# Channel shuffle: load and store buffers 3 + 2 against 2 + 3, with the first load and store buffer shared by the three small tiles

## Chip, cores, metric

One NeuronCore of a Trainium2 chip. The metric is the device time of the kernel in microseconds.

## The reference

`x` has shape (16, 64, 64, 256) in float32, `groups` is 8. Within each pixel the 256 channels are a matrix of 8 groups by 32 channels, and it is transposed. Nothing is calculated.

```python
def reference(x, groups):
    batch, h, w, c = x.shape
    x = x.reshape(batch, h, w, groups, c // groups)
    x = x.transpose(0, 1, 2, 4, 3)
    return x.reshape(batch, h, w, c)
```

67.11 MB are read and 67.11 MB written, whatever the kernel does.

## The kernel before

Each of the 128 partitions takes `q` pixels of 1 KB per tile, so a tile of 38 is a load of 38 KB a partition (4864 KB), one VectorE copy that permutes, and one store. Loads are issued by SyncE, stores by ScalarE. Small tiles of 4, 8 and 16 come first, so that the first store starts early.

```python
_SIZES = [4, 8, 16] + [38] * 12 + [28]
_IN_BUFS = 3
_OUT_BUFS = 2
# ... (pools of _IN_BUFS and _OUT_BUFS buffers)
    for q in _SIZES:
        in_tile = in_pool.tile([P, biggest * c], F32, name="in_tile")
        nc.sync.dma_start(out=in_tile[:, : q * c], in_=rows(x_flat, first, q))
        out_tile = out_pool.tile([P, biggest * c], F32, name="out_tile")
        nc.vector.tensor_copy(
            out=out_tile[:, : q * c].rearrange("p (i j g) -> p i j g", j=CPG, g=G),
            in_=in_tile[:, : q * c].rearrange("p (i g j) -> p i j g", g=G, j=CPG),
        )
        nc.scalar.dma_start(out=rows(out_flat, first, q), in_=out_tile[:, : q * c])
        first += P * q
```

Of the kernel before, what the change touches and what calls it, by code (L numbers as in the profile page):

```python
# [1 line left out]

# [4 lines left out]


F32 = mybir.dt.float32
P = 128  # L10

_SIZES = [4, 8, 16] + [38] * 12 + [28]
_IN_BUFS = 3
_OUT_BUFS = 2


@with_exitstack
def kernel(
    ctx: ExitStack,
    tc: tile.TileContext,  # L20
    x: bass.AP,
    groups: bass.AP,
    out: bass.AP,
):
    nc = tc.nc
    b, h, w, c = x.shape
    G = int(groups)
    CPG = c // G
    assert G * CPG == c
    assert sum(_SIZES) * P == b * h * w  # L30
    biggest = max(_SIZES)

    x_flat = x.rearrange("b h w c -> (b h w c)")
    out_flat = out.rearrange("b h w c -> (b h w c)")

    in_pool = ctx.enter_context(tc.tile_pool(name="in_pool", bufs=_IN_BUFS))
    out_pool = ctx.enter_context(tc.tile_pool(name="out_pool", bufs=_OUT_BUFS))

    def rows(flat, first, q):

        return flat[first * c : (first + P * q) * c].rearrange("(p f) -> p f", p=P)

    ctx.enter_context(tc.manual_schedule(engines=None))
    first = 0
    for q in _SIZES:
        in_tile = in_pool.tile([P, biggest * c], F32, name="in_tile")
        nc.sync.dma_start(out=in_tile[:, : q * c], in_=rows(x_flat, first, q))  # L47
        out_tile = out_pool.tile([P, biggest * c], F32, name="out_tile")
        nc.vector.tensor_copy(  # L49
            out=out_tile[:, : q * c].rearrange("p (i j g) -> p i j g", j=CPG, g=G),  # L50
            in_=in_tile[:, : q * c].rearrange("p (i g j) -> p i j g", g=G, j=CPG),
        )
        nc.scalar.dma_start(out=rows(out_flat, first, q), in_=out_tile[:, : q * c])
        first += P * q


# [1 line left out]
_INS = ['x', 'groups']  # L58
_OUTS = [((16, 64, 64, 256), 'float32')]

_NUMBERS = {'groups': 8}


# [26 lines left out]
```

## Time and profile before

| | before |
|---|---|
| time, median of the first 3 runs | 317.06 us (316.93 to 317.13) |
| span of the profiled run | 314.7 us |
| busy VectorE | 119.2 us, 38% |
| DMA engines, loads + stores | 49.8% + 49.4% of 16 engines' span |
| one round (one load, copy and store of 38 KB) | 23.0 us |

The page's DMA issues: tile and tensor, engine, count, KB each, median us from issue to landing.

```profile
in_tile<-in_x_dram SPq DMA_DIRECT2D x12, 4864.0 KB, 46.8
out_dram<-out_tile ACTq DMA_DIRECT2D x12, 4864.0 KB, 37.0
```

And the third copy (16 KB) in the timeline: start, length, instruction, and in brackets the idle time ahead of it with what ended it.

```profile
20.36 3.90 DVE L49 COPY out_tile<-in_tile 128x4096 f32<-128x4096 f32 x1 [11.75 <-DMA out_dram<-out_tile]
```

Its load had landed by 12.6 us (from the landings in the trace); it waited nearly 8 us more for an output buffer. This is the kind of wait that the change aims at.

### The profile page before, as it was taken

The page shows a single profiled execution, that of the slowest core. Times are in us where ns is not written, and L with a number is a line of the kernel's source. Part 1 is how long each engine was busy: PE and PEld are TensorE (multiplying, and loading weights), DVE is VectorE, ACT ScalarE, POOL GpSimd, SP SyncE. Part 2 cuts the span into 40 slices and gives each one's busy share as a digit, 9 for nine tenths or more (in the row PEclk, how much of TensorE's full clock was granted, in tenths as well). Part 3 has the DMA queues.
Part 4 walks back from the last instruction along what each step waited for, and adds up shares of the span by engine and source line. Part 5 has one row for each costly group of instructions (what it writes and reads, how often), then busy time and mean ns, then how long its engine had stood idle before and what let it go on. Part 6 is the DMA issues. An engine that isn't in the chain of part 4 may idle for free.

```text
span 314.7 us, 133 instructions
## 1 busy us (share of the span) xinstructions
DVE 119.2 (38%) x16; POOL 0.2 (0%) x4
## 2 busy tenths in 40 slices
DVE  3040645505506407407308209109109019046620
POOL 0000000000000000000000000000000000000000
DMA  8999999999999999999999999999999999999997
GB/s 308 452 398 454 413 419 466 396 475 396 455 415 445 425 430 440 425 445 415 455 396 470 401 465 406 460 411 460 411 460 411 460 411 455 428 395 454 455 418 306
DMA packets 4608, 134.22 MB, mean 427 GB/s; under 512 B 512, under 2 KB 512, under 8 KB 768
## 3 DMA queue, kind: packets, MB, share of 16 engines
q1 hardware_dynamic: 2304, 67.11, 49.8%
q10 hardware_dynamic: 2304, 67.11, 49.4%
HBM read 67.11 MB, written 67.11 MB: 427 GB/s over the span
## 4 chain that ended last, share of the span: by engine, by line
DMA 75%; DVE 20%; issue 0%; SPq 0%; DVEq 0%
DMA out_dram<-out_tile 74%; DVE out_tile L49 20%; DMA in_tile<-in_x_dram 2%; SPq L47 0%; DVEq L49 0%
## 5 line engine op out<-in xcount | busy, mean ns | idle before, releaser
L49 DVE COPY out_tile<-in_tile 128x9728 f32<-128x9728 f32 (+4 forms) x16 | 119.2, 7449 | 181.4 <-DMA out_dram<-out_tile 175.9
L71 POOL MEMSET const-bfloat16-1.0<- 128x1 bf16 x1 | 0.1, 102 | 0.0
L71 POOL MEMSET const-uint8-127<- 128x1 uint8 x1 | 0.1, 102 | 0.0
L71 POOL MEMSET const-float32-1.0<- 128x1 f32 x1 | 0.1, 99 | 0.0
L71 POOL MEMSET const-float32-0.0<- 128x1 f32 x1 | 0.1, 98 | 0.2 <-issue 0.2
## 6 DMA issues: line engine op xcount, KB each, us to landing
in_tile<-in_x_dram SPq DMA_DIRECT2D x12, 4864.0 KB, 46.8
out_dram<-out_tile ACTq DMA_DIRECT2D x12, 4864.0 KB, 37.0
in_tile<-in_x_dram SPq DMA_DIRECT2D x1, 3584.0 KB, 43.8
out_dram<-out_tile ACTq DMA_DIRECT2D x1, 3584.0 KB, 13.3
in_tile<-in_x_dram SPq DMA_DIRECT2D x1, 2048.0 KB, 11.0
out_dram<-out_tile ACTq DMA_DIRECT2D x1, 2048.0 KB, 26.7
in_tile<-in_x_dram SPq DMA_DIRECT2D x1, 1024.0 KB, 5.4
out_dram<-out_tile ACTq DMA_DIRECT2D x1, 1024.0 KB, 25.8
```

Of the source, the lines that this page charges most:

```text
L49: nc.vector.tensor_copy(out=out_tile[:, : q * c].rearrange("p (i j g) -> p i j g", j=CPG, g=G), in_=in_tile[:, : q * c].rearrange("p (i g ...
L71: nc = _bacc.Bacc("TRN2", target_bir_lowering=False, num_devices=1)
```

## The change

The intent: give a buffer to the store side, where VectorE waits, and take it from the load side; and let the three small tiles share one load buffer, so that two load buffers still let four loads start at once. Their outputs share one store buffer too. The total stays five buffers of 38 KB.

```diff
-_SIZES = [4, 8, 16] + [38] * 12 + [28]
-_IN_BUFS = 3
-_OUT_BUFS = 2
+_SLOTS = [[4, 8, 16]] + [[38]] * 12 + [[28]]
+_IN_BUFS = 2
+_OUT_BUFS = 3
 ...
-    for q in _SIZES:
+    for parts in _SLOTS:
         in_tile = in_pool.tile([P, biggest * c], F32, name="in_tile")
-        nc.sync.dma_start(out=in_tile[:, : q * c], in_=rows(x_flat, first, q))
         out_tile = out_pool.tile([P, biggest * c], F32, name="out_tile")
 ... (pieces: q, first row and columns of each part)
+        for q, start, cols in pieces:
+            nc.sync.dma_start(out=in_tile[:, cols], in_=rows(x_flat, start, q))
+        for q, start, cols in pieces:
+            nc.vector.tensor_copy(...)      # as before, on these columns
+            nc.scalar.dma_start(out=rows(out_flat, start, q), in_=out_tile[:, cols])
```

More of the change, by code (lines that the diff above doesn't have):

```diff
@@ L29 @@
     assert G * CPG == c
-    assert sum(_SIZES) * P == b * h * w
-    biggest = max(_SIZES)
+    assert sum(map(sum, _SLOTS)) * P == b * h * w
+    biggest = max(map(sum, _SLOTS))
     x_flat = x.rearrange("b h w c -> (b h w c)")
@@ L44 @@
     first = 0
-    for q in _SIZES:
+    for parts in _SLOTS:
         in_tile = in_pool.tile([P, biggest * c], F32, name="in_tile")
-        nc.sync.dma_start(out=in_tile[:, : q * c], in_=rows(x_flat, first, q))
         out_tile = out_pool.tile([P, biggest * c], F32, name="out_tile")
-        nc.vector.tensor_copy(
-            out=out_tile[:, : q * c].rearrange("p (i j g) -> p i j g", j=CPG, g=G),
-            in_=in_tile[:, : q * c].rearrange("p (i g j) -> p i j g", g=G, j=CPG),
-        )
-        nc.scalar.dma_start(out=rows(out_flat, first, q), in_=out_tile[:, : q * c])
-        first += P * q
+        at = 0
+        pieces = []
+        for q in parts:
+            pieces.append((q, first, slice(at * c, (at + q) * c)))
+            first += P * q
+            at += q
+        for q, start, cols in pieces:
+            nc.sync.dma_start(out=in_tile[:, cols], in_=rows(x_flat, start, q))
+        for q, start, cols in pieces:
+            nc.vector.tensor_copy(
+                out=out_tile[:, cols].rearrange("p (i j g) -> p i j g", j=CPG, g=G),
+                in_=in_tile[:, cols].rearrange("p (i g j) -> p i j g", g=G, j=CPG),
+            )
+            nc.scalar.dma_start(
+                out=rows(out_flat, start, q), in_=out_tile[:, cols]
+            )
 _INS = ['x', 'groups']
```

## The prediction

> **What bounds the kernel now.** I read the page's summary first, to see whether an engine or the DMA engines are full.
>
> ```profile
> span 314.7 us, 133 instructions
> DVE 119.2 (38%) x16; POOL 0.2 (0%) x4
> ...
> DMA  8999999999999999999999999999999999999997
> ...
> q1 hardware_dynamic: 2304, 67.11, 49.8%
> q10 hardware_dynamic: 2304, 67.11, 49.4%
> ```
>
> VectorE is idle 62% of the time. The DMA row has a 9 in every slice but the first and the last, and the two queues (q1 carries the loads, q10 the stores) together account for 49.8 + 49.4 = 99.2% of the time of all 16 DMA engines. To see what little is left I took the windows, cut where the stages change. Columns: stretch, its length, busy VectorE (instructions), busy POOL, clock, DMA share, GB/s.
>
> ```profile
> 0.00:1.70 1.70, 0.00 (x0) 0.20 (x4) 1.00 0.00 0
> 1.70:74.00 72.30, 24.51 (x6) 0.00 (x0) 1.00 1.01 429
> 74.00:258.20 184.20, 70.54 (x8) 0.00 (x0) 1.00 1.00 433
> 258.20:287.90 29.70, 17.42 (x2) 0.00 (x0) 1.00 1.01 438
> 287.90:313.20 25.30, 6.71 (x2) 0.00 (x0) 1.00 0.96 416
> 313.20:314.70 1.50, 0.00 (x0) 0.00 (x0) 1.00 0.00 0
> ```
>
> The DMA engines start at 1.7 us and are full until they finish at 313.2 us. In the steady stretch they move 433 GB/s. All 134.22 MB at 433 GB/s take 310.0 us; with 1.7 us ahead and 1.5 us behind that is 313.2 us, against a span of 314.7. So **no order of transfers of these sizes can win more than about 1.5 us, 0.5%**, unless it raises the rate itself.
>
> Then the waits, which look as though they said something else. Columns: engine, what waited, what for, us in total, times, longest.
>
> ```profile
> DVE out_tile L49 <- DMA out_dram<-out_tile: 175.9, 14, 14.6
> DVE out_tile L49 <- DMA in_tile<-in_x_dram: 5.5, 2, 4.1
> ...
> SPq L47 <- DVE out_tile L49: 224.4, 13, 22.2
> ```
>
> In 14 of 16 cases the copy has its input and waits for a store to give back an output buffer. This is the wait that a third store buffer takes away. But it is a wait of an engine that has 62% to spare, and the thing waited for is a store in a full queue. The chain of waits shows one round (start, length, what):
>
> ```profile
> 74.00 8.81 DVE out_tile L49
> 82.81 0.02 issue
> 82.83 37.45 DMA out_dram<-out_tile
> ...
> 120.36 8.91 DVE out_tile L49
> ```
>
> Two tiles take 120.36 - 74.00 = 46.36 us here, and 4 x 4.98 MB (two loads, two stores) in 46.36 us are 430 GB/s: the round is as long as its bytes need. The chain names the store only because the store is what the copy happens to be queued behind.
>
> **What the Trainium skill says.** "DMA: Bandwidth & Descriptors", section "Where 436 GB/s comes from", puts the ceiling of the 16 ports at 435.2 GB/s. The trace agrees: 433 in the steady stretch. "HBM Reference", section "Specifications (TRN2)", gives about 358 GB/s a core when both cores of a pair stream, and says that a core alone measures well above; 433 agrees with the second. "DMA: Bandwidth & Descriptors", section "Queues, rings and completion order", says that each DMA engine takes turns between the queues it has work for, packet by packet. The trace agrees: the 512 KB store of 4 KB rows took 15.1 us from issue to landing while the loads beside it had rows of 16 and 38 KB, where the 512 KB load alone took 3.3 us; and in the steady stretch loads and stores each get one tile per 23 us. "SBUF — State Buffer", section "SBUF size: 192, 224, or 256?", gives about 208 KiB per partition usable; before and after both hold 5 x 38 = 190 KB, so capacity does not change.
>
> **The change part by part.** The transfers keep their number (32), their sizes and their order within each queue. No copy is added or removed: VectorE keeps 16 copies and 119.2 us.
>
> *Third store buffer.* Copy i waited for store i-2, now for store i-3, one round (23.0 us) earlier. The wait was 14.2 us a round, so it goes, and the copy starts when its load lands. *Two load buffers.* Load i was issued when copy i-3 ended, now when copy i-2 ends: this takes depth from the load queue. *Shared first buffer.* The loads of 4, 8, 16 and the first 38 KB are issued at once; the fourth was issued at 5.2 us (after the 4 KB copy). The 28 KB rows ahead of it need 28 x 128 KB = 3.67 MB, or 8.5 us from 1.7 on, so it lay queued until 10 us: nothing is won. The first buffer comes free only after the copy of 16 KB.
>
> Are the DMA engines ever empty after the change? They are only if both queues are. (a) While a copy waits for its load, that load is moving. (b) While it waits for a store, that store is moving. (c) While it runs, 8.8 us: if a load freed it, the next load is queued already, since it was issued when the copy before ended, and takes 4.98 MB / 433 = 11.5 us even with the engines to itself; if a store freed it, the next store is queued behind, again 11.5 us. A new issue reaches the engines about 1 us after it (0.73 to 1.7 us at the start), so the worst case has 11.5 - 8.8 - 1.0 = **1.7 us to spare**, every round. With both queues non-empty throughout and turns taken packet by packet, every transfer lands when it landed before, whatever is queued when.
>
> From that the new schedule follows. Loads land as before, a store wait of 14.2 us ahead of the old copy, so copies move forward by about 14 us, the stores' issue with them, and stores take 37.0 + 13 to 14, about **50 us** to land; loads are issued one round later but by a copy 14 us earlier, 46.8 + 14.2 - 23.0 = about **38 us** to land. VectorE still idles about 181 us, now for the loads.
>
> The end: the last load lands at about 288 us (issue at 244.05, 43.8 to land). Its copy takes 6.5 us and no longer waits for the store before last (293.9 us), so the last store is issued at about 295 instead of 300.6. It follows the store of the last 38 KB tile, which has 4.98 + 3.67 MB with it from 293.9 on: 20 us, to 313.9. The last store was queued early enough before (300.6 + 1 against 313.9 - 8.5 = 305.4, 3.8 us to spare) and now is so by some 9 us. Earlier queuing moves nothing.
>
> Sum: start 0, steady stretch 0, end 0. **Predicted: 317.0 us.**
>
> **The rivals.**
>
> *1. Faster: the store wait is real.* Taking the 175.9 us of store waits as the limit, or even 14.2 us for each of 12 tiles, would promise 170 us. For it speaks the chain (74% of the span in stores). Against it the 1.00 in the DMA share. The windows allow 1.5 us: not below 315.5 us. *2. Two load buffers are too few.* If an issue reaches the engines later than 1 us, or a load is not yet issued when the copy starts, each of 13 rounds loses a piece of the 8.8 us copy; at 1 us a round it is 330 us, at the most (full copy exposed) 317 + 13 x 8.8 = 431. Against it the 1.7 us in the worst case, and that in the expected schedule the load is queued some 14 us before the one ahead lands. *3. The shared buffer orders its three parts one after the other.* If the program treats the buffer as a whole, the second copy waits for the first store out of the same output buffer, the third for the second. Loads of 4 + 8 + 16 + 38 rows (8.65 MB) and the first store (0.52 MB) keep the engines busy until 1.7 + 21.2 = 23 us; then only the 8 KB-row store is there (1.05 MB, 2.4 us), it lands near 26.5, the copy of 16 KB ends at 30.4, and only then do the next load and store come, at about 31.4: the engines idle for some 6 us, 323 us. If the first copy waits for all three loads too, the same steps give about 9.5 us, 326.5. For it: nothing in the trace of before can exclude it, as no buffer was shared. Against it: the three parts are separate columns, and a tracker that compares columns sees no conflict.
>
> **Range and chances.** The first two views bound the gain to 0.5% and the argument gives zero loss, so most of the weight is within a microsecond: the three runs of before span 316.93 to 317.13. I take 316.2 to 318.0 as the range. Rival 3 in its mild form (323 us) is still within 2%, in its hard form it is slower: 3%. Rival 2 adds 3% to slower. Faster by 2% (below 310.8 us) would need a rate over the ceiling: 1%. Same: 93%.
>
> **What would show it.** Right: a DMA row of nines as before and 433 GB/s in the middle; copies that wait for loads some 14 times, near 170 us in all, with hardly a wait for a store; a chain of loads instead of stores; median landing near 38 us for loads and 50 us for stores of 38 KB; the third copy starting near 12.7 us instead of 20.4; the last store issued near 295 us and landing near 314. Wrong: a slice of the DMA row below 9 in the middle (rival 2), or between 23 and 32 us with the second copy after the first store's landing (rival 3), or a rate in the middle other than 433 by over 1%, which would mean that the queues' depth changes the rate and that my zero is for the wrong reason.

## The result

| | before | after |
|---|---|---|
| median, 6 runs each of the same rounds | 317.0 us (316.43 to 317.15) | 316.26 us (316.18 to 316.29) |
| span of the profiled run | 314.7 us | 314.5 us |

The ratio is 0.9979, 95% interval 0.9966 to 0.9991: the same at 2%, as predicted, and 0.7 us lower. Ratios are the mean time of one kernel's fast runs over that of the other's of the same rounds, so not quite the ratio of the medians.

The page after: the DMA row, its two queues, and the chain that ended last by line.

```profile
DMA  8999999999999999999999999999999999999997
...
q1 hardware_dynamic: 2304, 67.11, 49.9%
q10 hardware_dynamic: 2304, 67.11, 49.4%
...
DMA in_tile<-in_x_dram 74%; DVE out_tile L57 19%; SPq L55 0%; DVEq L57 0%
```

The DMA row is the same digit for digit. The chain has turned round completely: loads have the 74% that stores had. The waits say the same.

```profile
DVE out_tile L57 <- DMA in_tile<-in_x_dram: 174.7, 16, 14.3
```

The 175.9 us of store waits are gone and VectorE now waits 174.7 us for loads. The windows, cut where they were cut before (stretch, length, busy VectorE, busy POOL, clock, DMA share, GB/s):

```profile
74.00:258.20 184.20, 70.99 (x8) 0.00 (x0) 1.00 1.00 433
258.20:287.90 29.70, 8.81 (x1) 0.00 (x0) 1.00 1.01 438
287.90:313.20 25.30, 6.58 (x1) 0.00 (x0) 1.00 0.96 416
313.20:314.70 1.50, 0.00 (x0) 0.00 (x0) 1.00 0.00 0
```

The same rates in the same stretches: 433, 438, 416. What did move is queueing time, in the issues and in the third copy:

```profile
in_tile<-in_x_dram SPq DMA_DIRECT2D x12, 4864.0 KB, 36.9
out_dram<-out_tile ACTq DMA_DIRECT2D x12, 4864.0 KB, 48.2
```

```profile
12.60 3.87 DVE L57 COPY out_tile<-in_tile 128x4096 f32<-128x4096 f32 x1 [4.04 <-DMA in_tile<-in_x_dram]
```

The third copy starts 7.8 us earlier; its store, issued earlier, simply lies in the queue for longer. Stores of 38 KB take 11.2 us more from issue to landing, loads 9.9 us less.

### The profile page after: what moved, and what is told of

Same layout as the page of the kernel before. It is cut to its first block, busy times and chain, and to the rows that moved or that the text cites. A ratio compares the mean times of both kernels' runs of the same rounds, so it can differ in the third digit from the quotient of the medians.

```text
span 314.5 us, 131 instructions
## 1 busy us (share of the span) xinstructions
DVE 120.0 (38%) x16; POOL 0.2 (0%) x4
## 4 chain that ended last, share of the span: by engine, by line
DMA 74%; DVE 19%; SPq 0%; issue 0%; DVEq 0%
DMA in_tile<-in_x_dram 74%; DVE out_tile L57 19%; SPq L55 0%; DVEq L57 0%
## 5 line engine op out<-in xcount | busy, mean ns | idle before, releaser
L57 DVE COPY out_tile<-in_tile 128x9728 f32<-128x9728 f32 (+4 forms) x16 | 120.0, 7501 | 174.7 <-DMA in_tile<-in_x_dram 174.7
## 6 DMA issues: line engine op xcount, KB each, us to landing
in_tile<-in_x_dram SPq DMA_DIRECT2D x12, 4864.0 KB, 36.9
out_dram<-out_tile ACTq DMA_DIRECT2D x12, 4864.0 KB, 48.2
```

What stands on the lines that cost most here:

```text
L57: nc.vector.tensor_copy(out=out_tile[:, cols].rearrange("p (i j g) -> p i j g", j=CPG, g=G), in_=in_tile[:, cols].rearrange("p (i g j) -> ...
```

## The experiments

My theory: the DMA engines are full in both kernels, so buffers only decide who waits. The rival: the waits, or the depth of a queue, are worth time. Kernels are compared only within the same rounds.

**Control.** The kernel before, unchanged.

> The kernel before once more, as a control for differences under 1 us. All theories: ratio 1.000, near 317.0 us. If its runs spread from 316.4 to 317.2 as before, the 0.7 us of the change is partly the spread of the kernel before; a ratio off 1.000 by over 0.1% would mean that such small differences cannot be read at all.

Measured 316.51 us against 316.81, ratio 0.9995 (0.9981 to 1.0009). The kernel before spread from 316.24 to 317.42 us. Its fastest runs are as fast as the changed kernel, so a few tenths of a microsecond between single runs here are scatter.

**The shared buffer alone.** Edit of the changed kernel:

```diff
-_IN_BUFS = 2
-_OUT_BUFS = 3
+_IN_BUFS = 3
+_OUT_BUFS = 2
```

> Shared first load buffer, but 3 load and 2 store buffers as before. My theory (the DMA engines are full, every transfer lands when it did): 316.2 to 317.2 us, and copies that wait for stores again, about 14 us a round. Theory X, that the 0.7 us gained come from the prologue: 316.3 us, ratio 0.998. Theory Y, that they come from the third store buffer: 317.0 us, ratio 1.000. Rival, that the store wait is on the path: no difference from before, since it is not removed.

Measured 316.49 us, ratio 0.999 (0.9976 to 1.0004), copies waiting 161.7 us for stores. The main theory holds; X and Y are 0.7 us apart and this run, between them, does not decide.

**The buffers alone, no sharing.** Edit of the kernel before:

```diff
-_IN_BUFS = 3
-_OUT_BUFS = 2
+_IN_BUFS = 2
+_OUT_BUFS = 3
```

> 2 load and 3 store buffers, no sharing. Mine: 316.2 to 317.2 us, copies wait for loads. Theory X (prologue): 317.0 us, ratio 1.000. Theory Y (third store buffer): 316.3 us, ratio 0.998. Rival, that sharing rescues a load queue that two buffers leave too shallow: slower than before by several us.

Measured **328.64 us**, ratio 1.0372 (1.0356 to 1.0388). My expectation missed by 11 to 12 us and the rival's "slower by several us" came true. But is it for the rival's reason, a load queue that runs dry? The same window of this kernel:

```profile
74.00:258.20 184.20, 66.48 (x8) 0.00 (x0) 1.00 1.00 412
```

The DMA share is still 1.00. The engines are not idle; they move 412 GB/s instead of 433. I come back to this below.

**Four buffers.** Edit of the changed kernel:

```diff
-_OUT_BUFS = 3
+_OUT_BUFS = 2
```

> After with only two store buffers, four buffers in all. Mine: the argument that one queue is never empty (11.5 us of the next transfer against an 8.8 us copy and 1 us of issue) needs no third buffer on either side, so 316.2 to 317.4 us, DMA row of nines, though copies wait for stores some 14 us a round. Rival 1 (a store wait costs time): slower than after by its 14 us x 12, up to 170 us. Rival 2 (two load buffers suffice only because the stores have three): slower by 1 to 8.8 us a round, 329 us or more.

Measured 316.3 us, ratio 0.9989 (0.9973 to 1.0006), one of six runs at 317.61. Waits and window:

```profile
DVE out_tile L57 <- DMA out_dram<-out_tile: 160.7, 12, 14.5
DVE out_tile L57 <- DMA in_tile<-in_x_dram: 19.1, 4, 9.5
```

```profile
74.00:258.20 184.20, 71.29 (x9) 0.00 (x0) 1.00 1.00 433
```

160.7 us of store waits are back and cost nothing. The fifth buffer, which the change moves from one side to the other, is not needed on either, once the first buffer is shared (without sharing, four buffers were not run). The third copy starts at 12.73 us here, with two store buffers: it is the sharing, and not the third store buffer, that takes away the early wait shown above.

**Each copy twice, before and after.** This takes the slack of the copy away (17.6 us instead of 8.8). In both kernels:

```diff
+    for _ in range(2):
         nc.vector.tensor_copy(...)
```

> Before, with each copy done twice (17.6 us a tile, 235 to 240 us of VectorE in all). Mine: no loss in the middle, since the next store was queued 23 us before it is needed and the copy's 17.6 us still fit. At the end the loads are out by 288 us, so only stores feed the DMA engines: copy 15th from 279.3 ends at 296.9, its store reaches the engines at 297.9 while the one before is through at 293.1 (4.8 us idle); the last copy then ends at 310.0, its store reaches them at 311.0 against 309.3 (1.7 us idle): 317.0 + 6.5, about 323.4 us. Rival, that copies are on the path of each round: + 12 x 8.8 = 106 us. Rival, that copies never matter: 317.0.

> After, with each copy done twice. Mine: copies start about 14 us earlier, so at the end the store of the 15th tile is issued at 285.8 (needed by 292) and the last at 301.2 + 1 = 302.2 (needed by 304.4): no idle, 316.3 us, thus some 7 us faster than before with copies twice. Rival, that the worst-case margin of 1.7 us is the one that counts: each of 12 rounds would lose 17.6 - 8.8 - 1.7 = 7 us, some 400 us. Rival, that copies are on the path: + 106 us.

Measured 338.65 us (ratio 1.068, 1.065 to 1.071) and 333.41 us (1.0523, 1.0503 to 1.0543). The order of the two kernels was as expected (5 us apart instead of 7), the sizes were not: 15 and 17 us more than I expected. Windows of before with copies twice (the last line is its end), then of after:

```profile
52.00:56.00 4.00, 4.00 (x2) 0.00 (x0) 1.00 0.72 311
...
74.00:258.20 184.20, 129.68 (x15) 0.00 (x0) 1.00 1.00 412
...
299.00:337.00 38.00, 27.41 (x4) 0.00 (x0) 1.00 0.71 304
```

```profile
42.00:46.00 4.00, 4.00 (x2) 0.00 (x0) 1.00 0.93 261
46.00:50.00 4.00, 4.00 (x1) 0.00 (x0) 1.00 0.79 340
...
74.00:258.20 184.20, 137.03 (x16) 0.00 (x0) 1.00 1.00 411
```

Two things show. The engines do run partly dry where two long copies follow each other at the start: a copy of 17.6 us is longer than the 11.5 us that the next transfer lasts, so the condition of the prediction fails there. At the end of before with copies twice they run partly dry again: share 0.71, an estimated 0.29 x 38 = 11 us of idle engines with the last 1 us of the program in it, where I had expected 6.5 us. And between start and end both kernels run at 411 to 412 GB/s with a share of 1.00, as the kernel without sharing did. In the steady stretch eight rounds of after with copies twice take 287.86 - 94.69 = 193.2 us (copy starts in the timeline), 24.1 us each instead of 23.0.

**One store buffer.** Edit of the changed kernel:

```diff
-_OUT_BUFS = 3
+_OUT_BUFS = 1
```

> After with one store buffer. Mine: now both queues run empty. A copy waits for the store just before; when it ends, the next load and the store start together, take 23 us, land, and during the next 8.8 us copy plus some 2 us of issue and landing nothing is queued: a round of about 34 us, 317 + 13 x 10.6 = about 455 us, DMA share near 0.68 in the middle. Rival, that waits of VectorE for stores never matter while it has 62% to spare: 317.

Measured 476.14 us, ratio 1.5019 (1.4983 to 1.5056). The DMA row, and one round of the chain:

```profile
DMA  8996495496496496496397397397397298195447
```

```profile
151.59 8.84 DVE out_tile L57
160.45 26.85 DMA out_dram<-out_tile
...
187.43 8.88 DVE out_tile L57
```

Here a store wait does cost time, because both queues are empty while the copy runs: the DMA row has holes in every round. A round is 187.43 - 151.59 = 35.8 us; I had 34, with a transfer pair at full rate. The missing 1.8 us are in slow packets, as in the kernels looked at below: load and store set off together, and over 100 to 250 us their packets of 38 KB take 1600 and 1509 ns on average instead of 1439, an estimated 8 x (161 + 70) ns = 1.8 us a round. So the same kind of wait, called by the same name in the waits, is free with two store buffers and costs 50% with one. What tells them apart is the DMA row, not the wait.

**No copies.** Wrong result, edit of the kernel before: the store reads the load buffer, five buffers, the same transfers.

```diff
-        out_tile = out_pool.tile(...)
-        nc.vector.tensor_copy(...)
-        nc.scalar.dma_start(out=rows(out_flat, first, q), in_=out_tile[:, : q * c])
+        nc.scalar.dma_start(out=rows(out_flat, first, q), in_=in_tile[:, : q * c])
```

> Wrong result on purpose: no copies, the store reads the load buffer, five buffers of 38 KB, same transfers. It measures what the transfers alone take. Mine: 315.5 to 316.5 us, so before and after lie within 1.5 us of the floor. Rival, that copies or their waits are on the path: well below, by up to the 175.9 us of store waits or the 119 us of copies.

Measured 316.23 us (316.14 to 316.31), ratio 0.998 (0.9962 to 0.9999). This is the floor of these transfers in this order, and the changed kernel, at 316.26, is on it. All copies and all their waits together are worth nothing in time.

**What the slow kernels have in common.** So three kernels at 412 GB/s, with the same bytes and full engines, had to be explained. The packet records of the trace hold queue, start, length and size of every packet; one packet is one partition's row, so a transfer has 128, 8 for each of the 16 engines (the records don't name the engine). I counted, over 100 to 250 us, by how many packets per engine the loads are ahead of the stores (the lead), how long packets of 38 KB take, and how many load packets per engine had begun when the first store's first packet began. Lengths are the median in ns, GB/s is from the window 74 to 258.2 us.

```
kernel                           begun  lead, mean  lead mod 8  load  store  GB/s
no copies                        18.9      18.2         2.2     1439   1439   433
four buffers                     21.0      19.1         3.1     1439   1439   433
after                            21.0      20.0         4.0     1439   1439   433
shared buffer alone              20.9      20.0         4.0     1439   1439   433
before                           21.0      20.2         4.2     1439   1439   433
buffers alone, no sharing        16.9      16.5         0.5     1439   1582   412
after, copies twice               -        16.5         0.5     1439   1582   411
before, copies twice              -        24.5         0.5     1439   1584   412
```

In these kernels the lead stays within two packets of what it was when the first store began, since load and store packets take turns (where copies are done twice it is set anew after the queues ran dry). Where it is 2 to 4 over a multiple of 8, both kinds of packet take 1439 ns. Where it is 0 to 1 over a multiple of 8, load and store are in step row by row, and every store packet takes about 145 ns more. The mean store packet there is 1588 ns: 8 x (1588 - 1439) = 1.2 us per transfer, which is the 24.1 instead of 23.0 us per round. In the kernel with the buffers alone the third load had to wait for the first copy and so was issued in the same moment as the first store (both at about 5.06 us): they set off in step. Sharing the first buffer puts the third and fourth load into the queue beforehand; the first store then falls into the middle of a load. This is a correlation found after the runs; four more kernels were to test it.

**A different lead with the buffers of after.** Edit of the changed kernel:

```diff
-_SLOTS = [[4, 8, 16]] + [[38]] * 12 + [[28]]
+_SLOTS = [[4, 8, 11]] + [[38]] * 12 + [[33]]
```

> After with 11 instead of 16 KB as the third part (the last tile 33 instead of 28). The packet records of the earlier runs show two kinds: where the loads are ahead of the stores by 18 to 21 packets an engine (2 to 5 more than a multiple of the 8 packets of one transfer), store packets of 38 KB take 1439 ns and the middle runs at 433 GB/s; where they are ahead by 16, 17, 24 or 25 (0 or 1 over a multiple of 8), they take about 1570 ns and it runs at 412. Phase theory: the lead is set by how many load packets are through when the first store starts, near 9 us; with 11 KB the first 38 KB load has just begun by then, the lead becomes 24 or 25, and the kernel falls to 412 GB/s, about 328 us, with two load and three store buffers, sharing and queues as in after. Rival, that the number of buffers or the sharing itself sets the rate: 316.3 us as after.

Measured 317.35 us (316.56 to 318.6), ratio 1.0018 (0.9991 to 1.0045), 433 GB/s. A miss, but of the lead and not of the rule: 22.8 load packets per engine had begun when the first store began, the mean lead became 21.9 (5.9 over 16), and store packets took 1439 ns. It adds a point to the fast side; it does not show that a changed lead makes this kernel slow.

**No sharing, another lead.** Edit of the kernel with the buffers alone:

```diff
-_SIZES = [4, 8, 16] + [38] * 12 + [28]
+_SIZES = [8, 34] + [38] * 12 + [14]
```

> Two load and three store buffers without sharing, as in the slow run of that kind, but the first transfers 8 and 34 KB (then 12 of 38 and 14), so that the first store starts in the middle of a load and not with one. Phase theory: lead near 13 to 14 packets (5 or 6 over 8): 433 GB/s in the middle, 316 to 317.5 us; if the lead should come out as 15 to 17 the run is slow and the theory is still held to its rule. Rival, that two load buffers without sharing are too few: 328 us or more at any lead.

Inconclusive. Four runs: 316.58, 336.21, 336.73 and 339.06 us; three lie over 1.5% above the fastest and count as slow. The only trace is of the 339.06 run, where the lead wanders from 14.2 to 17:

```profile
80.00:100.00 20.00, 8.72 (x1) 0.00 (x0) 1.00 1.00 424
...
140.00:180.00 40.00, 11.22 (x2) 0.00 (x0) 1.00 0.99 397
180.00:220.00 40.00, 17.65 (x2) 0.00 (x0) 1.00 1.01 408
```

Its packets tell more. Over 40 to 110 us the mean lead is 14.9 (6.9 over 8), loads of 38 KB take 1440 ns on average and stores 1490. At about 120 us the lead moves to 16.5, stays there, and over 120 to 260 us loads take 1544 and stores 1525 ns: with the same buffers the rate falls when the lead reaches a multiple of 8, though here load packets slow down as well. It also shows that a lead is not always kept; what moved it is open. The 316.58 us, one run, show that two load buffers without sharing can reach the floor, against that rival; that run was not traced.

**Output moved.** Wrong result: in the kernel with the buffers alone every tile but the last is written to another place of the output, those of 38 KB 2560 KB lower.

```diff
-        nc.scalar.dma_start(out=rows(out_flat, first, q), in_=out_tile[:, : q * c])
+        nc.scalar.dma_start(out=rows(out_flat, first + _SHIFT[q], q), in_=out_tile[:, : q * c])
```

> Wrong result on purpose: the slow kernel (2 load, 3 store buffers, no sharing), every 38 KB store written 2560 KB lower in the output, that is 67.4 rows of 38 KB, so that load and store beside each other no longer have addresses in HBM that lie whole tiles apart. Timing and lead as in the slow kernel. If the slow packets come from the addresses in HBM: back to 1439 ns, 433 GB/s, about 317 us. If they come from load and store using the same SBUF partitions at the same time: still about 1570 ns and 328.5 us.

Measured 328.64 us, ratio 1.0386 (1.0353 to 1.0419), lead 16.5, store packets 1578 ns, and

```profile
74.00:258.20 184.20, 65.89 (x8) 0.00 (x0) 1.00 1.00 412
```

Another distance in HBM between what is loaded and stored at one time did not change the rate; other distances were not tried.

**Stores in halves.** In the kernel with the buffers alone:

```diff
-        nc.scalar.dma_start(out=rows(out_flat, first, q), in_=out_tile[:, : q * c])
+        to = rows(out_flat, first, q)
+        nc.scalar.dma_start(out=to[64:], in_=out_tile[64:, : q * c])
+        nc.scalar.dma_start(out=to[:64], in_=out_tile[:64, : q * c])
```

> The slow kernel (2 load, 3 store buffers, no sharing) with each store cut into two of 64 partitions, the upper half first[...]. Bytes, packets and lead nearly the same, result right. If the slow packets come from the same partitions at the same time: 1439 ns for most packets, about 317 us. If from the addresses in HBM or from the lead as such: still 328.5 us, or in between.

Measured 373.8 us, ratio 1.1796 (1.1757 to 1.1835), slower than both expectations; one of its four runs was slow.

```profile
74.00:258.20 184.20, 61.93 (x7) 0.00 (x0) 1.00 1.00 387
```

The median packet is back at 1439 ns in both queues, but a quarter of the packets take over 1500 ns, and the means are 1556 (loads) and 1645 ns (stores). This does not answer the question: the number of stores changed too, the lead drifted from 20 to over 25, and no record says which partition a packet touches. That load and store in step touch the same SBUF partitions remains my best guess for the slow packets. It is argued, not shown.

None of the four kernels switched the rate by a lead that was set on purpose. The lead goes with the rate in every steady kernel above and within one trace; that it is the cause is likely, not shown.

## Why the prediction was right

*The bound.* Right, and shown from three sides: without any copy the same transfers take 316.23 us, with four buffers the store waits come back and the time does not change, and when a wait does empty both queues (one store buffer) the time follows at once.

*The measured 316.26 against 317.0 us.* Inside the range, but at its lower edge. I took the median of before for the floor; the floor is 316.2 and before has scatter on top of it. In the traces the DMA engines' last packet ends at 313.53 us before and at 313.31 after, while the last 16 packets end at 313.1 on average in both: what differs is a straggler. But the two traced runs are only 0.2 us apart (316.46 and 316.25), so this does not explain the 0.7. Whether the change as such removes this is open; the control and the kernel with the shared buffer alone differ from before by 0.1% or less and do not settle it.

*Never empty (1.7 us to spare).* Right for the kernel as predicted: the DMA row has its nines. Four buffers confirm the argument with one buffer less, and copies of 17.6 us show where it ends, at the start and at the end of the program.

*Every transfer lands when it did.* Right within 1.7 us: loads land within 0.2 us of where they did, stores up to 1.7 us earlier, for instance 141.6 against 143.2 us (from the landings in the trace), and 313.7 against 313.9 at the end.

*The new schedule.* Loads take 36.9 us to land (predicted about 38), stores 48.2 (about 50), the third copy starts at 12.60 (12.7), VectorE idles 174.7 us ahead of its copies (about 181), all 16 waits are for loads, and the last store is issued at 294.7 (295). The store's term was too large by the 1.6 to 1.7 us by which stores land earlier.

*Rival 1 (the store wait is real).* Wrong by the result, and by four buffers. *Rival 3 (parts in sequence).* Did not happen: the second copy starts at 6.54 us as its load lands. *Rival 2 (two load buffers too few).* Its time, not its mechanism, turned up: take away the sharing and the kernel is 12 us slower, though the load queue runs dry only once, from about 6 to 7 us, while the third load is on its way. The step of my argument that is not generally true is "with both queues non-empty ... every transfer lands when it landed before": it assumes that a packet takes the same time whatever runs beside it. The change keeps the lead of the loads at 20.0 packets (20.2 before), in the fast region, so the assumption held here. That is luck in part: I did not know of the lead and did not ask whether the change keeps it. I had treated the sharing as worth nothing ("nothing is won"). That is so against before; beside two load buffers it is worth 12 us, most likely because it keeps the first store from setting off in step with a load. A slip on which nothing rests: 2% below 317.0 us is 310.7, not 310.8.

## What to carry to other kernels

Look at the DMA row before believing a wait or a chain: with full queues in front of full DMA engines, more buffers only turn a wait for stores into a wait for loads, and the buffers are enough where a next transfer that outlasts the copy is always queued. A share of 1.00 is not the whole story, though: compare the GB/s as well, since the same queues can settle into a slower rhythm at the same share. Where two streams alternate, test the change of their start with both parts together and apart, since one part may be what keeps the other harmless.

## What the Trainium skill lacked or had wrong

- "DMA: Bandwidth & Descriptors", section "Where 436 GB/s comes from", has the HBM side (about 358 GB/s) bind for transfers between HBM and SBUF, though it adds that a measured 425 GB/s is near the fabric's rate. Loads and stores together ran at 433 GB/s here, with the other ceiling of that section (435.2) as the one that fits; "HBM Reference", section "Specifications (TRN2)", is closer to it.
- The same page, section "Queues, rings and completion order", describes taking turns by packets of some 9 to 17 descriptors. The records of this case alternate row by row: one packet of 38 KB of a load (1439 ns), then one of a store. Strung into 16 chains by their times, over 100 to 250 us a row follows a row of the same queue in 208 of 1648 steps after the change, once a transfer, and in none of 1569 in the kernel with the buffers alone. How many descriptors a record holds is not in the trace.
- No page that I read has the effect of the lead: store packets of 1582 ns instead of 1439 and 412 instead of 433 GB/s when load and store are in step row by row on each engine (lead 0 to 1 over a multiple of 8), and the full rate at 2 to 6. The cause is open.
- "DMA: Bandwidth & Descriptors", section "Latency and other measured facts", gives about 0.6 us to the first byte for DMAs issued as here, and does not say from where it counts. With idle engines the trace has 1.0 us from the start of the issuing instruction (0.73 to 1.73) and 0.6 from its end (1.10), which agrees. With loads queued the first store's first packet came 4.1 us after the start of its issue (5.17 to 9.25): the figure leaves out time in the queue.
